# One bank for a head's output and its transpose, separate tiles for transposed parts, other queue orders and a two-byte selection

## The chip, the cores and the metric

The kernel is one program on one core of a Trainium2 chip. The core has TensorE (PE, with its weight loads PEld), VectorE (DVE), ScalarE (ACT), GpSimd (POOL) and SyncE (SP), which issues most DMAs; each takes its own instructions in order. The metric is the device time of one execution in microseconds.

## The reference, cut to what matters

```python
h = rms_norm(x, norm_mix)                       # x is 1024 x 1024, f32
r_q, r_k, r_v, r_g, d_q, d_c, d_pe, d_g, i_q, i_k, i_w = split(h @ w_in)
r_q, r_k = rotary(r_q), rotary(r_k)             # 8 heads of 64, theta 1e4
ret = head_group_norm(retention(r_q, r_k, r_v)) * silu(r_g)
c_kv = rms_norm(d_c, kv_norm)                   # latent of 128
k_pe, q_pe = rotary(d_pe), rotary(d_q[..., :16])
q_idx, k_idx = partial_rotary(i_q), partial_rotary(i_k)   # 8 heads of 32
# per block of 128 rows: indexer, selection, attention
rel = relu(einsum('bthd,bsd->bths', q_idx, k_idx) * 32 ** -0.5)
score = where(key chunk <= query chunk, einsum('bth,bths->bts', i_w * 8 ** -0.5, rel), -inf)
top_val, top_idx = top_k(score, 256)
prob = softmax of the logits on the 256 chosen keys (8 heads)
dsa = (prob @ c_kv chosen) @ w_uv * silu(d_g)
x = x + concat(ret, dsa) @ w_out
x = x + sigmoid(rms_norm(x, norm_ple) @ w_ple_gate) * (p @ w_ple_proj)
return rms_norm(x, norm_final)
```

## The kernel before

The 1024 rows are eight tiles of 128. Operands of the large products are split into a high part that ACT rounds and a low part that DVE or POOL subtracts, and three products are summed in PSUM. Instructions of an engine stand in an order that a scheduler has worked out ahead of the run; `mark(name, ins)` names an instruction and `behind(ins, name)` puts another one behind it.

First the projection for rotation and indexer runs (to 40 us of the span). From 40 to 97 us DVE and ACT make the rotation tables (`tables`, L350 to L359: a first table cosx, sinx and a second cosr, sinr, each with four DVE steps, the ACT Sin of L356, two more ACT steps and the DVE step of L359, then times `rstd_b` at L446). DVE rotates the indexer's operands (L426), splits them (L427 on ACT, L428), and SP writes the parts `ih`, `il` (L415, L419) and `xs` (L435, L436) to DRAM tensors `d_iq` and `d_ik`, and the rotated keys and attention queries to `d_qs` and `d_kp` (L440, L442). SP then loads `ks` (L459) and for each tile `qs` (L464, L465) from there. Meanwhile PE works on projection chunks (`n_chunk`, L502 to L504: chunk 2, 3, then 0, 1 and later 4, 5); ACT copies their bank out as `nst` (L506) and that frees the bank.

From 97 to 172 us PE forms the indexer's scores (L477), ACT the relu (L480) and DVE the weighted sum into `sc` (L482, L484), tiles 7, 6, 4, 2, 3, 5 in turn. From there to 375 us each row's threshold is searched: `Rows` holds tiles 2, 3 and 5 under the name a, which DVE counts (L657), and tiles 7, 6 and 4 under c, which ACT counts by the Sign of L673, a count for each tile in each of 16 rounds, twice (on a 16-bit key and, after `narrow`, on the next 16 bits `place`). `choose` (L707 to L722) then makes the additive mask `bias` from the threshold with five DVE passes over the scores of a tile: equal (L718), a running count (L719), the first few equals (L720), greater plus those (L721), and the scaling to 0 and -1e30 (L722). PE has chunks 4 and 5 and retention's transposes beside it.

Attention runs from 375 to 625 us. `prep_k` (L768 to L779) and `prep_v` make keys `kk` and values `vd` per head; L956 forms logits in the banks `lg`, L958 adds `bias` and takes the maximum, L961 and L962 (exp) follow, `key_chunks` transposes the weights on PE (L979), splits them into a tile `t2` of two halves (ACT L985 for the high, DVE L986 for the low), and `by_dim` multiplies them with the values into an `oo` bank (L1014, L1015), copies that bank with ACT to `os` (L1017), and transposes `os` back into the other `oo` bank (L1020), from which DVE sums (L1021). Two banks carry the name `oo`, taken in turn. The order places retention's units between the heads. From 625 us the gate's product follows, with x transposed to `xT` tiles of two halves (L1189, L1190).

Of the kernel before, what the change touches and what calls it, by code (L numbers as in the profile page):

```python
# [153 lines left out]
def _body(ctx, nc, tc, ap, dbg):  # L154
# [5 lines left out]
    marks = {}  # L160

    def behind(ins, mark):

        marks.setdefault(mark, []).append(ins)
# [184 lines left out]
    def tables(cos_t, sin_t):  # L349
        ang, kk = cos_t, sin_t  # L350
        first = V.tensor_scalar(kk, ang, 1.0 / (2.0 * math.pi), MAGIC, op0=OP.mult, op1=OP.add)
        V.tensor_scalar(kk, kk, -MAGIC, None, op0=OP.add)
        for c in CODY:
            V.scalar_tensor_tensor(ang, kk, -c, ang, op0=OP.mult, op1=OP.add)
        last = V.tensor_scalar(ang, ang, PI_LO, -PI_LO, op0=OP.min, op1=OP.max)
        sin = A.activation(sin_t, ang, AF.Sin)  # L356
        A.activation(cos_t, ang, AF.Sin, scale=0.5)
        A.activation(cos_t, cos_t, AF.Square)
        V.tensor_scalar(cos_t, cos_t, -2.0, 1.0, op0=OP.mult, op1=OP.add)  # L359
        return first, last, sin  # L360

    with tc.issue_after(squares.ins):
        angles(1, cosx)
        _, reduced, sine = tables(cosx, sinx)
        turn = angles(0, cosr)
# [23 lines left out]
    spread(rstd_b, rstd, "chunk 2 tile 0")  # L389
# [33 lines left out]
    for h in range(2):  # L423
        sl = slice(512 * h, 512 * h + 512)
        ma, mb = rotate(P1[h], cosx, sinx, h)
        turned = V.tensor_tensor(out=xo[:, :, sl], in0=two(ma), in1=two(mb), op=OP.add)  # L426
# [33 lines left out]
    for i in TI:  # L460
# [4 lines left out]
        Y.dma_start(f(qs)[64:96], d_iq[0, :, :, tsl])  # L465
# [19 lines left out]
        V.memset(sc[0:64, so + w - 64:so + w], -3.0e38)  # L485
# [5 lines left out]
    def n_chunk(c, func, place=nb):  # L491
        ws = [load_w(ap["w_n"][c, kg], 256) for kg in range(4)]
        for tg in range(2):
            for a in range(4):
# [11 lines left out]
                A.activation(st[:, a % 2], pb[:, a % 2], func, scale=rstd[:, j:j + 1])  # L506
# [70 lines left out]
    spread(cq, rkv)  # L577
# [58 lines left out]
    class Rows:  # L636
# [70 lines left out]
        def choose(self):  # L707
# [5 lines left out]
            V.tensor_scalar(need, self.count(sc, kf_, OP.is_gt), -1.0, 256.0, op0=OP.mult, op1=OP.add)  # L713
            for n, i in enumerate(self.tiles):
# [6 lines left out]
                V.scalar_tensor_tensor(eq, sc[:, KS[i]], kf_[:, n:n + 1], eq, op0=OP.is_gt, op1=OP.add)  # L721
                V.tensor_scalar(bias[:, SL[i]], eq, 1.0e30, -1.0e30, op0=OP.mult, op1=OP.add)  # L722
# [11 lines left out]

    onV, onA = Rows([2, 3, 5], "a", False).steps(), Rows([7, 6, 4], "c", True).steps()
# [233 lines left out]
    def key_chunks(pt, s0, last, split):  # L969
# [36 lines left out]
    def by_dim(i, h, pt, od):  # L1006
        ot = bank("oo")[:, :256]
# [160 lines left out]
    def tail_in(j):  # L1168
# [14 lines left out]
        for q in range(2):  # L1183
            pt = bank("tp")
            for k in range(4):
                T.transpose(pt[:, 128 * k:128 * k + 128], xt[:, 512 * q + 128 * k:512 * q + 128 * k + 128], ident)
            x2 = (dw_.tile([128, 2, 512], FR, name="xT", tag="t2") if q else
                  dq_.tile([128, 2, 512], FR, name="xT", tag="ql"))
            A.activation(x2[:, 0], pt, AF.Copy)  # L1189
            V.tensor_tensor(out=x2[:, 1], in0=pt, in1=f(x2)[:, 0], op=OP.subtract)  # L1190
# [69 lines left out]
```

## Time and profile before

| what | us |
|---|---|
| median of 3 runs | 807.86 |
| lowest and highest run | 806.78, 809.04 |
| profiled execution | 805.41 |
| span of its instructions | 803.6 |
| PE busy in it | 754.4 |
| DVE busy | 582.0 |
| ACT busy | 469.4 |

The profile shows one execution: the span counts from the first instruction to the last, and the execution's own time is 1.81 us more. Busy time of PE counts overlapping matmuls and is modelled at its ends, so a PE that is busy is not a PE at its peak. A timeline has one row for each run of alike instructions of an engine, with its start and length, and in brackets how long the engine stood idle ahead of it and what ended that. The list of waits sums such times by the pair of waiting and releasing line.

### The profile page before, as it was taken

What the parts mean: (1) busy time and instruction counts of PE and PEld (TensorE: products, weight loads), DVE (VectorE), ACT (ScalarE), POOL (GpSimd) and SP (SyncE); (2) the same over time, 40 slices, a digit from 0 to 9 for tenths busy, and PEclk for the clock granted to TensorE, in tenths of its full rate; (3) what the DMA queues carried; (4) which work ended last, traced back from release to release, by engine and by line L of the source; (5) the groups of instructions that cost most, each with busy time, mean ns of one, the idle gap of its engine ahead of it and who ended that gap; (6) DMA issues with size and microseconds to landing.
All of it is one profiled execution on the core that took longest, in us unless ns stands there. A gap on an engine that the chain in (4) does not pass through costs nothing.

```text
span 803.6 us, 12584 instructions
## 1 busy us (share of the span) xinstructions
PE 754.4 (94%) x4415; PEld 656.1 (82%) x4415; DVE 582.0 (72%) x1254; ACT 469.4 (58%) x1025; POOL 311.9 (39%) x237
## 2 busy tenths in 40 slices
PE   9999699989999999998999989799999899999995
PEld 6888599879888887997888879588788687888885
DVE  4968489999997999999879778755754633255344
ACT  6543466729997899963756656744754321333232
POOL 2918325455666434710046557630312230411000
PEclk9999899999999999999999999999999999999998
DMA  9414815323333224604525454654533662131201
GB/s 317 122 28 127 240 48 131 91 55 94 117 117 119 80 66 135 210 28 131 131 66 153 159 150 115 207 174 108 178 123 91 220 211 95 61 112 66 79 26 53
DMA packets 60831, 97.11 MB, mean 121 GB/s; under 512 B 5376, under 2 KB 32384, under 8 KB 60768
## 3 DMA queue, kind: packets, MB, share of 16 engines
q1 hardware_dynamic: 57152, 89.76, 36.5%
q10 hardware_dynamic: 3616, 6.55, 2.3%
q8 instruction: 35, 0.57, 0.3%
q14 instruction: 28, 0.23, 0.1%
HBM read 67.06 MB, written 29.23 MB: 120 GB/s over the span
## 4 chain that ended last, share of the span: by engine, by line
PE 53%; DVE 20%; issue 11%; DMA 7%; POOL 4%; ACT 3%; SPq 2%; POOLq 0%; ACTq 0%; DVEq 0%
PE lg L1165 6%; PE ra L1165 5%; PE big L326 3%; PE big L325 3%; PE big L324 3%; PE oo L1165 3%; DVE res L657 3%; PE nb L502 2%; PE nb L503 2%; PE nb L504 2%; DMA qk<-d_f 2%; PE ra L1122 2%; PE ra L1123 2%; PE ra L1124 2%; DVE sc L484 2%
## 5 line engine op out<-in xcount | busy, mean ns | idle before, releaser
L237 POOL TENSOR_TENSOR wlo<-wraw,whi 128x512 fp32r<-128x512 f32 (+1 forms) x58 | 88.8, 1547 | 66.2 <-ACT whi L236 66.2
L673 ACT ACTIVATE ajunk<-key,cthr 128x1024 bf16<-128x1024 int16 (+5 forms) x96 | 95.5, 994 | 14.8 <-DVE key L634 10.5
L502 PE MATMUL nb<-whi,xhi 128*128 128x256 f32 x256 | 74.8, 295 | 8.8 <-ACT nst L506 8.8
L657 DVE TENSOR_SCALAR_CACHE_REDUCE res<-key,athr 128x384 f32<-128x384 int16 (+5 forms) x96 | 75.5, 786 | 2.1
L503 PE MATMUL nb<-wlo,xhi 128*128 128x256 f32 x256 | 74.1, 291 | 0.7 <-POOL wlo L237 0.7
L504 PE MATMUL nb<-whi,xlo 128*128 128x256 f32 x256 | 73.5, 290 | 0.0
L335 POOL TENSOR_TENSOR rs_y<-rs_a,mhalf 128x1 f32<-128x1 f32 (+1 forms) x26 | 26.2, 1006 | 101.5 <-DVE rs_a L334 98.7
L962 ACT ACTIVATE lm<-lm,mxv 128x896 f32<-128x896 f32 (+3 forms) x64 | 49.5, 775 | 25.6 <-DVE mxv L961 25.4
L985 ACT ACTIVATE t<-tp 128x512 fp32r<-128x512 f32 (+1 forms) x72 | 39.3, 556 | 39.5 <-PE oo L1015 27.1
L502 PEld LDWEIGHTS nb<-whi,xhi 128*128 128x128 f32 x256 | 50.7, 199 | 10.8 <-ACT nst L506 9.7
L325 PE MATMUL big<-xlo,whi 128*128 128x512 f32 x144 | 56.1, 389 | 0.0
L324 PE MATMUL big<-xhi,whi 128*128 128x512 f32 x144 | 55.7, 389 | 0.0
L986 DVE TENSOR_TENSOR t<-tp,t 128x512 fp32r<-128x512 f32 (+1 forms) x72 | 45.6, 640 | 14.0 <-ACT t L985 13.6
L326 PE MATMUL big<-xhi,wlo 128*128 128x512 f32 x144 | 55.7, 390 | 0.0
L484 DVE SCALAR_TENSOR_TENSOR sc<-rel,wi,sc 128x1024 f32<-128x1024 f32 (+5 forms) x42 | 51.0, 1213 | 5.8 <-ACT rel L480 3.1
L958 DVE CUSTOM_DVE_ANT_0 lm<-lg,bias 128x512 f32<-128x512 f32 (+2 forms) x64 | 36.7, 587 | 23.5 <-PE tp L979 12.0
L503 PEld LDWEIGHTS nb<-wlo,xhi 128*128 128x128 f32 x256 | 50.8, 199 | 1.9 <-POOL wlo L237 1.3
L504 PEld LDWEIGHTS nb<-whi,xlo 128*128 128x128 f32 x256 | 50.4, 198 | 0.6
L979 PE MATMUL tp<-cst,lm 128*128 128x128 f32 x288 | 48.1, 277 | 0.6 <-DVE rs_a L334 0.3
L1014 PE MATMUL oo<-t,vd 128*128 128x256 f32 (+1 forms) x144 | 40.5, 293 | 7.7 <-ACT os L1017 6.2
L1219 DVE SCALAR_TENSOR_TENSOR sqx<-sqx,oo 128x512 f32<-128x512 f32 (+1 forms) x17 | 10.5, 653 | 49.6 <-PE oo L1165 35.0
L236 ACT ACTIVATE whi<-wraw 128x512 fp32r<-128x512 f32 (+1 forms) x58 | 34.9, 609 | 14.9 <-POOL cg L535 4.2
(492 smaller groups left out, 2423.5 us busy)
## 6 DMA issues: line engine op xcount, KB each, us to landing
wraw<-in_w_t SPq DMA_DIRECT2D x26, 256.0 KB, 2.7
wraw<-in_w_n SPq DMA_DIRECT2D x24, 256.0 KB, 2.6
d_f<-o SPq DMA_DIRECT2D x8, 512.0 KB, 3.9
qk<-d_f SPq DMA_DIRECT2D x8, 512.0 KB, 4.5
ql<-d_qs SPq DMA_DIRECT2D x16, 256.0 KB, 5.1
qh<-d_qs SPq DMA_DIRECT2D x32, 128.0 KB, 4.1
twr<-in_w_out SPq DMA_DIRECT2D x8, 512.0 KB, 5.4
xt<-in_x SPq DMA_DIRECT2D x8, 512.0 KB, 3.5
```

The lines of the kernel that those rows point to most:

```text
L237: G.tensor_tensor(out=lo, in0=raw, in1=f(hi), op=OP.subtract)
L324: T.matmul(outs[h], wh, xhi[k][:, sl], start=k == 0, stop=False)
L325: T.matmul(outs[h], wh, xlo[k][:, sl], start=False, stop=False)
L326: last = T.matmul(outs[h], wl, xhi[k][:, sl], start=False, stop=k == 7)
L484: V.scalar_tensor_tensor(dst, rel[:, :w], wi[:, i, h:h + 1], dst, op0=OP.mult, op1=OP.add)
L502: T.matmul(pb[:, a % 2], xhi[k][:, tsl], wh, start=k == 0, stop=False)
L503: T.matmul(pb[:, a % 2], xhi[k][:, tsl], wl, start=False, stop=False)
L504: last = T.matmul(pb[:, a % 2], xlo[k][:, tsl], wh, start=False, stop=k == 7)
L657: V.tensor_scalar(junk, src[:, KS[i]], thr[:, n:n + 1], 0.0, op0=op, op1=OP.add, accum_out=cnt[:, n:n + 1])
L673: A.activation(junk[:, :128 * (i + 1)], src[:, KS[i]], AF.Sign, bias=self.thr[:, n:n + 1], accum_out=cnt[:, n:n + 1])
L962: A.activation(lm[:, :w], lm[:, :w], AF.Exp, bias=mx, scale=0.125, accum_out=den[:, a, h:h + 1])
L1165: T.matmul(po[c.start // 512][:, c.start % 512:c.start % 512 + c.stop - c.start], a, b[:, c], start=k == 0 and m == 0, stop=k == n - 1 and ...
```

## The change

- The stores of `xs` to `d_qs` and `d_kp` and part of the DRAM work stand behind the load of the first tile's queries on SP ("first queries").
- The second table's first DVE step stands behind the last `xs` subtract; its Sin stands behind the last copy of chunk 3 ("chunk 3 copied 7"); its last three DVE steps stand behind the scoring of tile 4 ("scored 4").
- `spread` of rstd stands behind tile 1 of chunk 2 (it was tile 0), and that of the kv norm behind "block 10".
- One Sign of the first round (tile 6) stands behind a copy of chunk 1.
- In `choose` the count of the greater ones writes its 0 or 1 as bf16 into the memory of `key`; L721, which compared f32 scores again, becomes an add of two bf16 tiles (L730 in the new file), and L722 leaves DVE for an ACT Identity (new L731) with `out_of`, a column of -1e30 that one POOL memset fills.
- `by_dim` takes one bank for a head: the output in columns 0 to 255, the transpose in 256 to 511; `os` is 256 wide. `t2` becomes three tiles `th` and two tiles `tl`; three of the `xT` pairs in the tail use them.

DVE has six scaled compares fewer and six adds more, and six scalings fewer; ACT has six more; PE and SP have as many instructions as before.

```diff
     def behind(ins, mark):
-        marks.setdefault(mark, []).append(ins)
+        if mark in marked:
+            queue(ins, marked[mark])
+        else:
+            marks.setdefault(mark, []).append(ins)
...
-    spread(rstd_b, rstd, "chunk 2 tile 0")
+    spread(rstd_b, rstd, "chunk 2 tile 1")
...
-        (V if h else G).tensor_tensor(out=xs[1][:, :, sl], in0=xo[:, :, sl], in1=f(xs[0])[:, :, sl], op=OP.subtract)
+        parts = (V if h else G).tensor_tensor(out=xs[1][:, :, sl], in0=xo[:, :, sl], in1=f(xs[0])[:, :, sl], op=OP.subtract)
...
-            Y.dma_start(d_qs[n, :, 8 * x:8 * x + 8].rearrange("b j h t -> (j h) b t"),
-                        f(xs[n])[0:64, x].rearrange("p (b t) -> p b t", t=256))
-        Y.dma_start(d_kp[n].rearrange("(x j) t -> j x t", x=2), f(xs[n])[104:112])
-    first, *_ = tables(cosr, sinr)
-    queue(first, turned)
+            behind(Y.dma_start(d_qs[n, :, 8 * x:8 * x + 8].rearrange("b j h t -> (j h) b t"),
+                               f(xs[n])[0:64, x].rearrange("p (b t) -> p b t", t=256)), "first queries")
+        behind(Y.dma_start(d_kp[n].rearrange("(x j) t -> j x t", x=2), f(xs[n])[104:112]), "first queries")
+    first, _, sine, cosine = tables(cosr, sinr)
+    queue(first, parts)
+    behind(sine, "chunk 3 copied 7")
+    behind(cosine, "scored 4")
     for t in (cosr, sinr):
-        V.tensor_tensor(out=t, in0=t, in1=rstd_b, op=OP.mult)
+        behind(V.tensor_tensor(out=t, in0=t, in1=rstd_b, op=OP.mult), "scored 4")
...
-    spread(cq, rkv)
+    spread(cq, rkv, "block 10")
...
+                    if bit == 15 and n == 1 and src is key:
+                        behind(ins, "chunk 1 copied 3")
...
+            above = key.bitcast(BF)
-            V.tensor_scalar(need, self.count(sc, kf_, OP.is_gt), -1.0, 256.0, op0=OP.mult, op1=OP.add)
+            V.tensor_scalar(need, self.count(sc, kf_, OP.is_gt, above), -1.0, 256.0, op0=OP.mult, op1=OP.add)
...
-                V.scalar_tensor_tensor(eq, sc[:, KS[i]], kf_[:, n:n + 1], eq, op0=OP.is_gt, op1=OP.add)
-                V.tensor_scalar(bias[:, SL[i]], eq, 1.0e30, -1.0e30, op0=OP.mult, op1=OP.add)
+                V.tensor_tensor(out=above[:, KS[i]], in0=above[:, KS[i]], in1=eq, op=OP.add)
+                A.activation(bias[:, SL[i]], above[:, KS[i]], AF.Identity, scale=1.0e30, bias=out_of)
...
-        t2 = dw_.tile([128, 2, 512], FR, name="t2")
-        th, tl_ = t2[:, 0], t2[:, 1]
+        th = tl_ = dw_.tile([128, 512], FR, name="th", bufs=3)
         if split:
+            tl_ = dw_.tile([128, 512], FR, name="tl")
...
-        ot = bank("oo")[:, :256]
+        both = bank("oo")
+        ot = both[:, :256]
...
-        os_ = dw_.tile([128, 512], F32, name="os")[:, :256]
+        os_ = dw_.tile([128, 256], F32, name="os")
         A.activation(os_, ot, AF.Copy)
-        tbp = bank("oo").rearrange("p (j d) -> p j d", d=128)
+        tbp = both[:, 256:].rearrange("p (j d) -> p j d", d=128)
```

The first place is SP's queue between the last `d_iq` store of the low parts and the first queries `qs`. Before:

```order
26 L415 DMA d_iq<-il 64x1024
27 L419 DMA d_ik<-il 24x1024
28 L440 DMA d_qs<-xs_520 64x4x256 x2
29 L442 DMA d_kp<-xs_520 8x2x1024
30 L459 DMA ks<-d_ik 32x1024 x3
31 L521 DMA d_g_88<-nst 128x2x128
32 L521 DMA d_g_89<-nst 128x2x128
33 L415 DMA d_iq<-ih 128x1024
34 L521 DMA d_g_88<-nst 128x2x128
35 L521 DMA d_g_89<-nst 128x2x128
36 L233 DMA wraw<-in_w_n 128x512
37 L464 DMA qs<-d_iq 64x8x128
```

Now, where L418, L422, L464, L469, L470 and L443 are the old L415, L419, L459, L464, L465 and L440:

```order
26 L418 DMA d_iq<-il 64x1024
27 L422 DMA d_ik<-il 24x1024
28 L464 DMA ks<-d_ik 32x1024 x2
29 L469 DMA qs<-d_iq 64x8x128
30 L464 DMA ks<-d_ik 32x1024
31 L470 DMA qs<-d_iq 32x8x128
32 L443 DMA d_qs<-xs_519 64x4x256 x2
33 L445 DMA d_kp<-xs_519 8x2x1024
34 L443 DMA d_qs<-xs_520 64x4x256 x2
35 L445 DMA d_kp<-xs_520 8x2x1024
```

Nine DMAs and the three `ks` loads stood between the low parts' stores and the first queries' load; now only the `ks` loads do, one of them between its two halves. The six stores to `d_qs` and `d_kp`, which all stood ahead of the queries, now come behind them, and the `ih` store of row 33 stands ahead of the piece shown.

The second place is ACT's queue in the last three rounds of the second search (`ajunk` is the Sign's output, `cthr` and `csg` its small steps). Before, from the 896 wide Sign of the third round from the end:

```order
440 L673 ACTIVATE ajunk,ccnt<-key,cthr 128x896
441 L676 ACTIVATE csg<-ccnt,coff 128x1
442 L836 ACTIVATE kk_4552<-qk 128x512
443 L841 ACTIVATE qz_4555<-qk 64x4x128 x2
444 L506 ACTIVATE nst<-lg,rstd 128x256
445 L524 DMA d_dg<-nst 128x2x256
446 L673 ACTIVATE ajunk,ccnt<-key,cthr 128x640
447 L676 ACTIVATE csg<-ccnt,coff 128x1
448 L678 ACTIVATE cthr<-csg,cthr 128x1
```

Now, with L679 the Sign and L731 the new Identity:

```order
429 L731 ACTIVATE bias<-key,out_of 128x384
430 L684 ACTIVATE csg<-ccnt,coff 128x1
431 L679 ACTIVATE ajunk,ccnt<-key,cthr 128x896
432 L530 DMA d_dg<-nst 128x2x256
433 L512 ACTIVATE nst<-ra,rstd 128x256
434 L731 ACTIVATE bias<-key,out_of 128x512
435 L686 ACTIVATE cthr<-csg,cthr 128x1
436 L679 ACTIVATE ajunk,ccnt<-key,cthr 128x640
437 L684 ACTIVATE csg<-ccnt,coff 128x1 x2
438 L679 ACTIVATE ajunk,ccnt<-key,cthr 128x1024
439 L686 ACTIVATE cthr<-csg,cthr 128x1
440 L731 ACTIVATE bias<-key,out_of 128x768
```

The masks of tiles 2, 3 and 5 (384, 512 and 768 wide) now stand between the Signs of c, the last of them with two Signs of its round and the whole last round behind it.

The third place is DVE's queue at the end of the selection of tile 4 (640 wide), where the first key products `kk` are subtracted. Before:

```order
377 L718 TENSOR_SCALAR junk<-sc,ckfin 128x640
378 L719 SCALAR_TENSOR_TENSOR res<-junk 128x640
379 L720 SCALAR_TENSOR_TENSOR junk<-res,cneed,junk 128x640
380 L721 SCALAR_TENSOR_TENSOR junk<-sc,ckfin,junk 128x640
381 L722 TENSOR_SCALAR bias<-junk 128x640
382 L779 TENSOR_TENSOR kk_4365<-oo,kk_4365 64x512
383 L779 TENSOR_TENSOR kk_4365<-tp,kk_4365 64x512
```

Now, where L727 to L730 are the old L718 to L721 and L790 the old L779:

```order
379 L727 TENSOR_SCALAR junk<-sc,ckfin 128x640
380 L728 SCALAR_TENSOR_TENSOR res<-junk 128x640
381 L790 TENSOR_TENSOR kk_4361<-oo,kk_4361 64x512
382 L790 TENSOR_TENSOR kk_4361<-tp,kk_4361 64x512
383 L729 SCALAR_TENSOR_TENSOR junk<-res,cneed,junk 128x640
384 L790 TENSOR_TENSOR kk_4362<-oo,kk_4362 64x512
385 L790 TENSOR_TENSOR kk_4362<-tp,kk_4362 64x512
386 L730 TENSOR_TENSOR key<-key,junk 128x640
```

The subtracts of the first two heads' keys move ahead of the last one or two steps of the selection.

## Rows read from the trace of the kernel before

**Rows 1.** The page's head and its totals: busy time, share of the span and instructions.

```profile
span 803.6 us, 12584 instructions
PE 754.4 (94%) x4415; PEld 656.1 (82%) x4415; DVE 582.0 (72%) x1254; ACT 469.4 (58%) x1025; POOL 311.9 (39%) x237
```

**Rows 2.** Stretches of the span: length, then busy time and instructions of PE, PEld, DVE, ACT and POOL, granted clock of TensorE, DMA share, GB/s.

```profile
40.00:97.00 57.00, 46.90 (x331) 43.88 (x330) 38.48 (x35) 23.84 (x35) 28.71 (x20) 0.97 0.46 123
...
375.00:530.00 155.00, 140.85 (x953) 125.16 (x953) 125.89 (x315) 99.84 (x186) 76.21 (x69) 0.96 0.51 150
```

**Rows 3.** What PE waited for over the whole span: line and releaser, us in total, times, longest.

```profile
PE nb L502 <- ACT nst L506: 8.8, 3, 5.1
PE oo L1014 <- ACT os L1017: 6.2, 4, 3.2
...
PE oo L760 <- DVE kk L779: 2.3, 1, 2.3
...
PE ib L371 <- issue: 1.6, 1, 1.6
```

**Rows 4.** Timelines of PE and ACT between 78 and 98 us: start, length, engine and line.

```profile
84.78 0.58 PE L502 MATMUL nb<-whi,xhi 128*128 128x256 f32 x1 [5.08 <-ACT nst L506]
96.71 1.17 PE L477 MATMUL big<-ks,qs 96*128 96x512 f32 x4 [3.20 <-DMA qs<-d_iq]
```

```profile
83.31 1.06 ACT L356 ACTIVATE sinr<-cosr 128x1024 f32<-128x1024 f32 x1 [5.36 <-DVE cosr L355]
```

**Rows 5.** Timeline of DVE between 69 and 98 us.

```profile
69.99 2.89 DVE L351 TENSOR_SCALAR sinr<-cosr 128x1024 f32<-128x1024 f32 x1
...
72.92 1.67 DVE L352 TENSOR_SCALAR sinr<-sinr 128x1024 f32<-128x1024 f32 x1
74.51 3.42 DVE L428 TENSOR_TENSOR xs<-xo,xs 128x1024 fp32r<-128x1024 f32 x1
...
84.39 1.23 DVE L446 TENSOR_TENSOR sinr<-sinr,rstd_b 128x1024 f32<-128x1024 f32 x1 [1.12 <-ACT sinr L356]
88.07 0.94 DVE L359 TENSOR_SCALAR cosr<-cosr 128x1024 f32<-128x1024 f32 x1 [2.45 <-ACT cosr L358]
89.05 2.20 DVE L446 TENSOR_TENSOR cosr<-cosr,rstd_b 128x1024 f32<-128x1024 f32 x1
```

**Rows 6.** SP's queue of DMAs between 80 and 93 us, and POOL's `il`, which its first row stores.

```profile
80.53 0.92 SPq L415 DMA_DIRECT2D d_iq<-il  x1
...
87.95 0.49 SPq L415 DMA_DIRECT2D d_iq<-ih  x1
...
91.24 0.56 SPq L464 DMA_DIRECT2D qs<-d_iq  x1
91.84 1.13 SPq L465 DMA_DIRECT2D qs<-d_iq  x1
```

```profile
74.00 2.85 POOL L252 TENSOR_TENSOR il<-it,ih 128x1024 fp32r<-128x1024 f32 x1
```

**Rows 7.** The end of the scoring: length, DVE's busy time and instructions, granted clock, DMA share, GB/s.

```profile
150.00:172.00 22.00, 21.81 (x23) 1.00 0.33 91
```

**Rows 8.** Timeline of DVE in the selection: tiles 2, 3 and 5 of a, then 7, 6 and 4 of c, and the first key subtract.

```profile
339.93 1.57 DVE L721 SCALAR_TENSOR_TENSOR junk<-sc,akfin,junk 128x384 bf16<-128x384 f32 x1
...
345.59 0.75 DVE L721 SCALAR_TENSOR_TENSOR junk<-sc,akfin,junk 128x512 bf16<-128x512 f32 x1
...
352.24 1.94 DVE L721 SCALAR_TENSOR_TENSOR junk<-sc,akfin,junk 128x768 bf16<-128x768 f32 x1
...
354.49 0.16 DVE L683 TENSOR_SCALAR cv<-cthr 128x3 int32<-128x3 f32 x1
...
362.57 1.28 DVE L721 SCALAR_TENSOR_TENSOR junk<-sc,ckfin,junk 128x1024 bf16<-128x1024 f32 x1
363.89 0.43 DVE L722 TENSOR_SCALAR bias<-junk 128x1024 bf16<-128x1024 bf16 x1
...
372.05 0.89 DVE L720 SCALAR_TENSOR_TENSOR junk<-res,cneed,junk 128x640 bf16<-128x640 f32 x1
372.97 0.89 DVE L721 SCALAR_TENSOR_TENSOR junk<-sc,ckfin,junk 128x640 bf16<-128x640 f32 x1
373.89 0.33 DVE L722 TENSOR_SCALAR bias<-junk 128x640 bf16<-128x640 bf16 x1
374.25 0.69 DVE L779 TENSOR_TENSOR kk<-oo,kk 64x512 fp32r<-64x512 f32 x1
```

**Rows 9.** Timeline of ACT in the last three rounds of c: the Signs by width and the last small step.

```profile
337.88 1.03 ACT L673 ACTIVATE ajunk<-key,cthr 128x896 bf16<-128x896 uint16 x1
...
341.28 0.82 ACT L673 ACTIVATE ajunk<-key,cthr 128x640 bf16<-128x640 uint16 x1
...
344.51 1.03 ACT L673 ACTIVATE ajunk<-key,cthr 128x896 bf16<-128x896 uint16 x1
...
352.93 0.48 ACT L678 ACTIVATE cthr<-csg,cthr 128x1 f32<-128x1 f32 x2
```

**Rows 10.** Attention: PE's timeline at two heads' starts, and from ACT's list of waits between 375 and 640 us the weight split of L1064 (line and releaser, us in total, times, longest).

```profile
411.74 0.39 PE L1014 MATMUL oo<-t,vd 128*128 128x256 f32 x1 [1.51 <-ACT os L1017]
...
473.99 0.39 PE L1014 MATMUL oo<-t,vd 128*128 128x256 f32 x1 [0.90 <-ACT os L1017]
```

```profile
ACT wo3h L1064 <- DMA twr<-in_w_out: 2.9, 1, 2.9
```

More of the change, by code (lines that the diff above doesn't have):

```diff
@@ L172, in mark @@
     def mark(name, ins):
+        marked[name] = ins
         for x in marks.pop(name, []):
@@ L358, in tables @@
         A.activation(cos_t, cos_t, AF.Square)
-        V.tensor_scalar(cos_t, cos_t, -2.0, 1.0, op0=OP.mult, op1=OP.add)
-        return first, last, sin
+        return first, last, sin, V.tensor_scalar(cos_t, cos_t, -2.0, 1.0, op0=OP.mult, op1=OP.add)
     with tc.issue_after(squares.ins):
         angles(1, cosx)
-        _, reduced, sine = tables(cosx, sinx)
+        _, reduced, sine, _ = tables(cosx, sinx)
         turn = angles(0, cosr)
@@ L425, in _body @@
         ma, mb = rotate(P1[h], cosx, sinx, h)
-        turned = V.tensor_tensor(out=xo[:, :, sl], in0=two(ma), in1=two(mb), op=OP.add)
+        V.tensor_tensor(out=xo[:, :, sl], in0=two(ma), in1=two(mb), op=OP.add)
         A.activation(xs[0][:, :, sl], xo[:, :, sl], AF.Copy)
-        (V if h else G).tensor_tensor(out=xs[1][:, :, sl], in0=xo[:, :, sl], in1=f(xs[0])[:, :, sl], op=OP.subtract)
+        parts = (V if h else G).tensor_tensor(out=xs[1][:, :, sl], in0=xo[:, :, sl], in1=f(xs[0])[:, :, sl], op=OP.subtract)
         pw = big()
@@ L464, in _body @@
         Y.dma_start(f(qs)[0:64], d_iq[:, :, :, tsl].rearrange("n r h t -> (n r) h t"))
-        Y.dma_start(f(qs)[64:96], d_iq[0, :, :, tsl])
+        mark("queries" if i != TI[0] else "first queries", Y.dma_start(f(qs)[64:96], d_iq[0, :, :, tsl]))
         so = OFF[i] - OFF[2]
@@ L484, in _body @@
                 V.scalar_tensor_tensor(dst, rel[:, :w], wi[:, i, h:h + 1], dst, op0=OP.mult, op1=OP.add)
-        V.memset(sc[0:64, so + w - 64:so + w], -3.0e38)
+        mark(f"scored {i}", V.memset(sc[0:64, so + w - 64:so + w], -3.0e38))
     ix.close()
@@ L505, in n_chunk @@
                 mark(f"chunk {c} tile {j}", last)
-                A.activation(st[:, a % 2], pb[:, a % 2], func, scale=rstd[:, j:j + 1])
+                mark(f"chunk {c} copied {j}",
+                     A.activation(st[:, a % 2], pb[:, a % 2], func, scale=rstd[:, j:j + 1]))
                 if a % 2 == 0:
@@ L651, in start, with count @@
             G.memset(self.thr, -at if self.scalar else at)
-        def count(self, src, thr, op):
+        def count(self, src, thr, op, out=None):
             cnt = self.small("cnt")
             for n, i in enumerate(self.tiles):
-                junk = tkp.tile([128, S], F32, name="res")[:, :128 * (i + 1)]
+                junk = tkp.tile([128, S], F32, name="res")[:, :128 * (i + 1)] if out is None else out[:, KS[i]]
                 V.tensor_scalar(junk, src[:, KS[i]], thr[:, n:n + 1], 0.0, op0=op, op1=OP.add,
@@ L672, in bit @@
                     junk = tkp.tile([128, S], BF, name="ajunk", bufs=1)
-                    A.activation(junk[:, :128 * (i + 1)], src[:, KS[i]], AF.Sign, bias=self.thr[:, n:n + 1],
-                                 accum_out=cnt[:, n:n + 1])
+                    ins = A.activation(junk[:, :128 * (i + 1)], src[:, KS[i]], AF.Sign, bias=self.thr[:, n:n + 1],
+                                       accum_out=cnt[:, n:n + 1])
+                    if bit == 15 and n == 1 and src is key:
+                        behind(ins, "chunk 1 copied 3")
                 for n in range(self.n):
@@ L733, in steps @@
                 yield
+    out_of = tkp.tile([128, 1], F32, name="out_of", bufs=1)
+    G.memset(out_of, -1.0e30)
     onV, onA = Rows([2, 3, 5], "a", False).steps(), Rows([7, 6, 4], "c", True).steps()
@@ L987, in key_chunks @@
         else:
-            th = f(t2)[:, s0 // 2 % 2]
+            th = f(th)
             A.activation(th[:, :o], tp[:, :o], AF.Copy)
@@ L1186, in tail_in @@
                 T.transpose(pt[:, 128 * k:128 * k + 128], xt[:, 512 * q + 128 * k:512 * q + 128 * k + 128], ident)
[L1187 to L1190, printed above, removed]
+            if q:
+                xh, xl = (dw_.tile([128, 512], FR, name="xT" + tag, tag=tag, bufs=n) for tag, n in (("th", 3), ("tl", 2)))
+            else:
+                x2 = dq_.tile([128, 2, 512], FR, name="xT", tag="ql")
+                xh, xl = x2[:, 0], x2[:, 1]
+            A.activation(xh, pt, AF.Copy)
+            V.tensor_tensor(out=xl, in0=pt, in1=f(xh), op=OP.subtract)
             for k in range(4):
-                hi.append(x2[:, 0, 128 * k:128 * k + 128])
-                lo.append(x2[:, 1, 128 * k:128 * k + 128])
+                hi.append(xh[:, 128 * k:128 * k + 128])
+                lo.append(xl[:, 128 * k:128 * k + 128])
         return xt, sq, r1, p2, hi, lo
```

2 lines of the change are left out of this document (1 added, 1 removed).

## The prediction

> **What bounds the kernel now.** I read the totals first: PE is busy for 754.4 of 803.6 us [rows 1], so a change that only spares DVE or ACT work pays where PE, or what PE comes to wait for, is held by it. [...] The third is the list of what PE waits for: 8.8 us for ACT's copy of a chunk bank, 6.2 us for `os`, 2.3 us for the first key subtract, 1.6 us for the issue of the spread of rstd [rows 3]. The timelines tell what those waits hang on, and here the reader should look at who stood in front of the releaser. ACT's Sin was idle 5.36 us for DVE's last table step and began at 83.31; the copy that PE needed stood behind it, so PE stood 5.08 us until 84.78. Then PE came to the first score and stood 3.20 us more for the queries, until 96.71 [rows 4]. At the end of the scoring DVE is busy 21.81 of 22.00 us, so DVE sets that end [rows 7]. In the selection of c DVE works without a hole from 354.49, just behind ACT's last small step at 352.93 [rows 9], to the key subtract at 374.25 [rows 8] that ends PE's wait.
>
> **Up to the first score.** Two DVE steps of the second table, 2.89 and 1.67 us, ran ahead of the `xs` subtract [rows 5]; they now follow it. With the four stores of the second halves gone from the front of SP's queue, the last part the queries need is `il`. It ended at 76.85 (74.00 plus 2.85), but its store was issued only at 80.53 [rows 6]. The spread of rstd now follows one more tile of chunk 2; it waited 1.6 us anyway, and I let `il` come 1 us later, at 77.9. Its two stores are then issued to about 79.4, the second from 78.8. From issue of a store to the load that waits for it took 3.3 us (87.95 to 91.24), and from the second queries' load to the first score 4.87 us (91.84 to 96.71) [rows 4, 6]. So 78.8 + 3.3 + 0.7 for the `ks` load in between + 4.9 gives 87.7. PE itself, free of the 5.08, 3.20 and 1.6 us, would be there at 86.8, so nothing earlier is to be had but by the clock. The first score moves by 9.0 us; from one more landing (6) to the earlier PE with its clock held (11).
>
> **What that costs later.** DVE's last three table steps leave a stretch where it was idle for a stretch where it is the bound: 0.94, 1.23 and, for the second product, 1.23 to 2.20 us [rows 5], 3.4 to 4.4 in all; I take 4. The Sin and its two followers fall into ACT time that has holes in the scoring. So the scoring ends, and both searches begin, 9 - 4 = 5 us earlier. A wait for a copy behind a Sign (in the other 3.7 of the 8.8 us in rows 3) may go as well, but what ends the selection is not PE, so I count it at nothing. The other spread ("block 10") has about as many transposes in front of it as before: nothing.
>
> **The selection.** Two things run against each other. First, ACT. The three masks of a now stand between the Signs of c. In the old times ACT comes to the first at 337.9 (the 896 Sign) and must wait until DVE's step at 339.93 is done, say 340.5; the mask itself costs about 0.6 us, between nothing and the 0.82 of the 640 wide Sign [rows 8, 9]. That is 3.2 us. The second waits for a step that began at 345.59, now about 1.7 us sooner, where ACT is at 344.5: 0.9 us more. The third stands ahead of the 896 Sign that began at 344.51 and is at its place at about 348.5, and waits for the step that began at 352.24, sooner by the savings on the first two tiles (1.3 + 0.3 + 0.4 + 0.3), so near 350.6; with its own 0.9 us that Sign begins at 351.5, 7.0 us late. Behind it are the rest of that round and one whole round, 344.51 to 353.4: ACT ends near 360.4 and DVE's `cv` begins 6.0 us late, at 360.5. Second, DVE's own chain from `cv` to the key subtract, 19.76 us, loses the three scalings (0.43 + about 0.4 + 0.33), saves on three adds, and has the last L720 (0.89) and the last add behind the subtract [rows 8]. No row shows an add of two bf16 tiles: it lies between a scaling (0.43 at 1024 wide) and the compare that it replaces (1.28). I take half the compare, since it has two tensor inputs as that has and two bytes as the scaling has: 3.3 us becomes 1.7. So 19.76 - 1.1 - 1.6 - 1.3 = 15.8, and the subtract begins at 376.3 on the old clock, 2.0 us later than before. If ACT never waited it would be 4.0 us earlier; at the old prices of the compares and with every step of a as slow as before, 6.8 later (`cv` near 364.3 and 16.8 of chain). [...]
>
> **Attention and tail.** Of the 6.2 us that PE waited for `os`, two waits (1.51, 0.90) are a head whose first product needs the bank that the head before still holds [rows 3, 10]. With a bank of its own for every head in turn this is gone, since the transpose no longer takes the second bank. The longest, 3.2 us, is not of this kind alone: ACT stood 2.9 us for a DMA of `wo3` [rows 10], ahead of its copy; the next head no longer needs that copy, but transposes of the old head do, so I count it only in the bound. That makes 3.0 us. The clock's 0.96 over 155 us [rows 2] is some 6 us; which of its falls follow these waits the rows don't tell, and I give a third, 2 us. So 5 us, from nothing (the next wait, the maximum of the logits, stands right behind) to 9. Three `th` tiles against two pairs spare ACT waits, not PE's. The `xT` tiles in the tail: nothing, as PE has work there and waits for other lines.
>
> **The sum.** The profiled execution took 805.41 us; 805.4 - 9 + 4 + 2 - 5 = 797.4. The median of the runs is 2.45 us above that execution, so 799.9 by it.
>
> **Rivals.** *The gain comes whole.* ACT's masks don't hold the Signs, because DVE's a steps come sooner than I make them or ACT had slack, and all `os` waits go with their clock falls: 805.4 - 11 + 3.4 - 4 - 9 = 784.8, median 787.3. For it: two of the three compares of a, 1.57 and 1.94 us, stand far above what their width asks [rows 8], and adds may not; against it: the order in which ACT's rows stand. *The banks change nothing.* In attention each wait for `os` is followed by a wait for the next logits, and the time goes there: 802.4, median 804.9, which a measurement can hardly tell from no change. *Slower: the masks hold ACT's queue.* One mechanism, at 338 to 351 us: ACT takes its instructions in order, and a mask that waits for DVE stops the Signs, whose end DVE then waits for. At the upper price the key subtract comes 6.8 us late; it decides as soon as the first score's lead, less the tables, is under that: with 6 - 4.4 = 1.6 of lead and an attention that gains nothing, 805.4 - 1.6 + 6.8 = 810.6, median 813.1. The compare of 384 wide that took 1.57 us against 0.75 for 512 wide [rows 8] shows that a DVE step there can cost twice its price, which feeds this case. [...]
>
> **How the numbers follow.** Forecast 0.50, whole gain 0.22, no gain from the banks 0.16, slower 0.12. About 0.3% (2.4 us) is what a measurement of this kernel can tell from no change, so faster means below 805.4. Faster: nearly all of the first two and half of the third, 0.79; same: the rest of the third and the edge of the others, 0.10; slower 0.11. The range runs from 786, which cuts off the better half of the whole gain (some 0.10), to 808, which cuts off most of the slower case (0.10).
>
> **What would show it.** The first score near 88 us in place of 96.71, with no ACT Sin ahead of it; the three DVE table steps after tile 4's scoring; an end of the scoring 5 us earlier. In the selection three holes in ACT of some 2.6, 0.3 and 2 us ahead of the masks, and a hole on DVE ahead of `cv`; adds of 1024 wide between 0.43 and 1.28 us. In attention the pair of L1014 and `os` gone from PE's list of waits, and the clock above 0.96. I am wrong if the queries land no earlier, if ACT shows no hole there, or if the attention's stretch is as long as before.

## The result and the profile after

| what | before | after |
|---|---|---|
| median of 4 runs, us | 807.32 | 797.37 |
| lowest and highest | 804.48, 809.04 | 794.67, 799.03 |
| span of the profiled execution | 803.6 | 797.2 |

The ratio is 0.987, with a 95% interval from 0.982 to 0.992: about 10 us faster, clear of noise, and 2.5 us from the 799.9 that was forecast. The two profiled executions, 805.41 and 799.03 us, lie 6.4 us apart, so the stages below account for that much. But the stages did not share the time out as forecast. Three points of the two traces show it: PE's first key product, the last logits, and the end. One execution of experiment 1, the profiled one, ran at a granted clock of 0.65 and took 1038.33 us; it is left out of the times below.

Timeline of PE before, the first key product and the last logits (its wait is in [rows 3]):

```profile
375.00 0.79 PE L760 MATMUL oo<-uvh,ckh 128*128 128x512 f32 x1 [2.26 <-DVE kk L779]
...
620.87 0.28 PE L957 MATMUL lg<-kk,ql 128*128 128x256 f32 x1
```

The same two after the change:

```profile
381.90 0.50 PE L771 MATMUL oo<-uvh,ckh 128*128 128x512 f32 x1 [2.26 <-DVE kk L790]
...
614.75 0.29 PE L968 MATMUL lg<-kk,ql 128*128 128x256 f32 x1
```

Up to the key product the changed kernel loses 6.9 us. From there to the last logits it takes 232.85 us (614.75 less 381.90) instead of 245.87, so it wins 13.0. From there to the end it takes 182.5 us instead of 182.7. The sum is the 6.4 us between the spans.

**The start.** Timeline of PE after the change, in the stretch that ends with the first score:

```profile
50.93 0.58 PE L507 MATMUL nb<-whi,xhi 128*128 128x256 f32 x1 [3.46 <-ACT nst L512]
...
56.21 1.56 PE L374 MATMUL ib<-cst,rstd 128*128 128x128 f32 x11
...
92.84 1.16 PE L482 MATMUL big<-ks,qs 96*128 96x512 f32 x4 [1.14 <-DMA qs<-d_iq]
```

The old waits of 5.08 and 3.20 us [rows 4] are gone or down to 1.14, yet the first score is only 3.9 us earlier. The first row is new: the chunk matmuls that now stand ahead of the spread (the second row) need a bank that ACT copies out with rstd as its scale. PE waits 3.46 us for that copy, and then runs them at a granted clock of 0.50, from 52 to 56 us. The stretches (columns as in [rows 2]) show it and, at the end of the scoring, DVE still the bound:

```profile
40.00:97.00 57.00, 51.64 (x356) 48.39 (x356) 34.82 (x32) 22.43 (x32) 30.26 (x21) 0.94 0.38 105
...
52.00:56.00 4.00, 4.00 (x21) 4.00 (x20) 0.00 (x0) 0.00 (x0) 0.00 (x0) 0.50 0.00 0
...
150.00:172.00 22.00, 21.52 (x166) 20.62 (x165) 21.72 (x24) 8.81 (x18) 17.26 (x9) 1.00 0.27 90
375.00:530.00 155.00, 144.01 (x1020) 130.12 (x1019) 134.05 (x336) 109.85 (x205) 78.93 (x70) 0.99 0.54 160
```

The three table steps in the scoring (timeline of DVE after) cost 0.62 + 2.06 + 1.21, that is 3.9 us:

```profile
135.12 0.62 DVE L363 TENSOR_SCALAR cosr<-cosr 128x1024 f32<-128x1024 f32 x1
135.67 2.06 DVE L451 TENSOR_TENSOR sinr<-sinr,rstd_b 128x1024 f32<-128x1024 f32 x1
137.98 1.21 DVE L451 TENSOR_TENSOR cosr<-cosr,rstd_b 128x1024 f32<-128x1024 f32 x1
...
168.37 0.11 DVE L490 MEMSET sc<- 64x64 f32 x1
```

The last row ends the scoring. Before it was

```profile
169.12 0.11 DVE L485 MEMSET sc<- 64x64 f32 x1
```

so 0.75 us are left of the lead.

**The selection.** Timeline of ACT after: a Sign of the third round from the end, and the masks of tiles 2, 3 and 5 (compare [rows 9]):

```profile
339.30 1.13 ACT L679 ACTIVATE ajunk<-key,cthr 128x1024 bf16<-128x1024 uint16 x1
...
345.73 0.62 ACT L731 ACTIVATE bias<-key,out_of 128x384 bf16<-128x384 bf16 x1 [2.28 <-DVE key L730]
...
349.95 0.72 ACT L731 ACTIVATE bias<-key,out_of 128x512 bf16<-128x512 bf16 x1 [2.03 <-DVE key L730]
...
354.76 0.93 ACT L731 ACTIVATE bias<-key,out_of 128x768 bf16<-128x768 bf16 x1 [1.40 <-DVE key L730]
```

Each mask stopped ACT for DVE, 5.7 us in all. Timeline of DVE after (compare [rows 8]):

```profile
345.35 0.34 DVE L730 TENSOR_TENSOR key<-key,junk 128x384 bf16<-128x384 bf16 x1
...
365.78 0.17 DVE L691 TENSOR_SCALAR cv<-cthr 128x3 int32<-128x3 f32 x1 [11.06 <-ACT cthr L686]
...
373.68 0.69 DVE L730 TENSOR_TENSOR key<-key,junk 128x1024 bf16<-128x1024 bf16 x1
...
381.15 0.69 DVE L790 TENSOR_TENSOR kk<-oo,kk 64x512 fp32r<-64x512 f32 x1
```

DVE, which had no hole here before, stands 11.06 us for ACT's last small step. Its own chain is short: 15.4 us from `cv` to the key subtract, where it was 19.76, and an add 1024 wide takes 0.69 us.

**Attention.** PE's list of waits between 375 and 530 us (columns as in [rows 3]), the wait for the maximum `mxv` before:

```profile
PE lg L956 <- DVE mxv L958: 3.7, 4, 1.7
```

and the list after:

```profile
PE oo L1026 <- ACT th L996: 2.9, 2, 1.5
PE oo L771 <- DVE kk L790: 2.8, 2, 2.3
PE ra L888 <- DVE x L867: 1.8, 3, 0.9
...
PE lg L967 <- DVE mxv L969: 0.8, 2, 0.4
```

The pair with `os`, 6.2 us of [rows 3], is gone, the clock is 0.99 in place of 0.96 (last stretch above), and there is a second change: the wait of the logits for `mxv` is 0.8 us in place of 3.7. The stretches from key product to last logits, before and after (columns as in [rows 2]):

```profile
375.00:620.87 245.87, 230.61 (x1503) 203.43 (x1504) 175.42 (x476) 146.91 (x307) 92.46 (x80) 0.97 0.47 141
```

```profile
381.90:614.75 232.85, 224.12 (x1506) 200.25 (x1507) 173.06 (x482) 149.04 (x311) 92.78 (x80) 0.99 0.49 148
```

PE's idle time falls from 15.3 to 8.7 us and the busy time of as many matmuls from 230.6 to 224.1, at a granted clock of 0.99 in place of 0.97: half of the 13.0 us is less waiting, half is shorter busy time.

### The profile page after: what moved, and what is told of

It is laid out like the page before. It is cut to its first block, busy times and chain, and to the rows that moved or that the text cites. A ratio compares the mean times of both kernels' runs of the same rounds, so it can differ in the third digit from the quotient of the medians.

```text
span 797.2 us, 12581 instructions
## 1 busy us (share of the span) xinstructions
PE 752.3 (94%) x4415; PEld 656.7 (82%) x4415; DVE 576.9 (72%) x1248; ACT 474.1 (59%) x1031; POOL 314.0 (39%) x238
## 4 chain that ended last, share of the span: by engine, by line
PE 39%; DVE 7%; DMA 5%; ACT 2%; issue 1%; POOL 0%; SPq 0%; POOLq 0%; DVEq 0%
PE lg L1177 6%; PE ra L1177 5%; PE ra L1136 3%; PE ra L1134 3%; PE ra L1135 3%; PE oo L1177 3%; PE tp L990 3%; PE lg L967 2%; PE lg L968 1%; PE oo L1027 1%; PE oo L1026 1%; DMA twr<-in_w_gate 1%; PE ra L904 1%; DVE qz L853 1%; DMA d_mix<-og 1%
## 5 line engine op out<-in xcount | busy, mean ns | idle before, releaser
L679 ACT ACTIVATE ajunk<-key,cthr 128x1024 bf16<-128x1024 int16 (+5 forms) x96 | 95.4, 993 | 16.0 <-DVE key L640 9.5
L996 ACT ACTIVATE th<-tp 128x512 fp32r<-128x512 f32 (+1 forms) x72 | 40.0, 558 | 38.5 <-PE tp L990 37.3
L973 ACT ACTIVATE lm<-lm,mxv 128x896 f32<-128x896 f32 (+3 forms) x64 | 49.5, 774 | 22.4 <-DVE mxv L972 20.1
L997 DVE TENSOR_TENSOR tl<-tp,th 128x512 fp32r<-128x512 f32 (+1 forms) x72 | 45.8, 639 | 7.4 <-ACT th L996 5.0
L1026 PE MATMUL oo<-th,vd 128*128 128x256 f32 (+1 forms) x144 | 40.5, 289 | 2.9 <-ACT th L996 2.9
L1027 PE MATMUL oo<-tl,vd 128*128 128x256 f32 (+1 forms) x144 | 40.2, 312 | 0.0
```

Source lines behind the costliest of these rows:

```text
L679: ins = A.activation(junk[:, :128 * (i + 1)], src[:, KS[i]], AF.Sign, bias=self.thr[:, n:n + 1], accum_out=cnt[:, n:n + 1])
```

## The experiments

Times are medians; the kernel before ran beside each group (806.4, 807.8 and 806.9 us). Line numbers are those of each kernel.

**1. The spread.** In the changed kernel, one word:

```diff
-    spread(rstd_b, rstd, "chunk 2 tile 1")
+    spread(rstd_b, rstd, "chunk 2 tile 0")
```

> The changed kernel with one edit taken back: the spread of rstd stands behind tile 0 of chunk 2 again. Theory: tile 1 first needs a bank that ACT copies out only when rstd is known, so the spread (56.21 us in the changed kernel, 49.39 before) came 6.8 us late and pushed all vector work of this stage; with tile 0 the spread is near 49.4, the first score 5 to 7 us earlier than 92.84, the scoring ends near 162, and the time falls by 4 to 7 us below the changed kernel's 797.4, to 790.5 to 793.5. Rival: SP's stores and loads set the first score, not the vector work; then it stays within 1.5 us of 92.84 and the time within 2 us of 797.4.

Measured: 794.0 us, ratio to before 0.984 (0.982 to 0.986). That is 3.4 us under the changed kernel: the theory's direction, less than its 4 to 7. The stages are read in another kernel with the same edit:

**2. The early part alone**, with the spread behind tile 0; the choice and the attention are those of before. SP's order, the Sign behind chunk 1 and the spread of the kv norm behind "block 10" are in it too; none of them was tried by itself.

> The changed kernel with the choice and the attention of before, and the spread of rstd behind tile 0: the early part alone, without its worst step. Theory: the first score comes 5 to 8 us before 96.7, the scoring ends 2 to 5 us earlier (the table steps on DVE take 3.4 to 4.4 back), and the time is 802 to 804.5. Rival: what is won up to the scoring is lost in the two searches, whose ACT order changes with it; then within 2.4 us of 806.4.

Measured: 802.93 us, ratio 0.995 (0.992 to 0.998). Timelines of PE and of DVE in it:

```profile
49.39 0.79 PE L374 MATMUL ib<-cst,rstd 128*128 128x128 f32 x5 [1.66 <-issue]
...
88.10 1.17 PE L482 MATMUL big<-ks,qs 96*128 96x512 f32 x4 [1.01 <-DMA qs<-d_iq]
```

```profile
163.92 0.11 DVE L490 MEMSET sc<- 64x64 f32 x1
...
372.39 0.69 DVE L787 TENSOR_TENSOR kk<-oo,kk 64x512 fp32r<-64x512 f32 x1
```

The spread is 6.8 us earlier than in the changed kernel (49.39 against 56.21), the first score 4.7 (88.10 against 92.84) and the scoring ends 5.2 before that of the kernel before. At the first key subtract 1.9 us are left of it (372.39 against 374.25 in [rows 8]). So the spread set the first score, as the theory had it (8.6 us before that of the kernel before, a little over its 8), and the time is the theory's; but most of the lead is lost in the searches, as the rival had it, though not by ACT's order.

The trace shows where. `cv` follows DVE's search of a without a hole, as before (353.91 against 354.49), so DVE sets it; ACT's search is done 1.8 us earlier. From the end of the scoring to the end of that search (the second `av`, 335.25 against 334.55) DVE takes 171.3 us where it took 165.4. The search has one small step `ad` in each of its 32 rounds. DVE's list of lines (count, us in total, mean ns, idle) before and in this run:

```profile
L666 DVE TENSOR_SCALAR ad<-acnt 128x3 bf16<-128x3 f32 x32 | 14.0, 438 | 0.7
```

```profile
L672 DVE TENSOR_SCALAR ad<-acnt 128x3 bf16<-128x3 f32 x32 | 19.8, 620 | 0.8
```

The median of these steps is 0.17 us in both. The 11 of this run that took more than 0.4 us all stood beside a POOL instruction and ended within 0.04 us of the end of one, such as this pair of timelines:

```profile
206.23 1.85 DVE L672 TENSOR_SCALAR ad<-acnt 128x3 bf16<-128x3 f32 x1
```

```profile
205.64 2.41 POOL L541 TENSOR_TENSOR cg<-cosr,gam 128x1024 f32<-128x1024 f32 x1
```

The new order puts more of them there: the 32 steps take 19.4 to 20.1 us in all seven kernels that have the early part (the changed one, experiments 2, 3 and 8 to 11) and 14.0 to 15.8 in the five without it. That POOL's work holds these steps is read from the rows; no run moved that work away.

**3. The masks.** In the changed kernel the three masks are put behind c's search:

```diff
-                    A.activation(new[:, n:n + 1], sg[:, n:n + 1], AF.Identity, scale=-half, bias=self.thr[:, n:n + 1])
+                    ins = A.activation(new[:, n:n + 1], sg[:, n:n + 1], AF.Identity, scale=-half, bias=self.thr[:, n:n + 1])
+                if bit == 0 and src is place:
+                    mark("searched", ins)
...
-                A.activation(bias[:, SL[i]], above[:, KS[i]], AF.Identity, scale=1.0e30, bias=out_of)
+                ins = A.activation(bias[:, SL[i]], above[:, KS[i]], AF.Identity, scale=1.0e30, bias=out_of)
+                if not self.scalar:
+                    behind(ins, "searched")
```

> The changed kernel with the three ACT masks of tiles 2, 3 and 5 put behind the last small step of c's search; the work is the same, only ACT's order differs. Theory: the masks held the Signs; without them ACT has no wait for a key of L730 before 358 us, DVE's cv comes 6 to 8 us sooner than 365.78, the key subtract near 374, and the time falls by 4 to 7 us, to 790.5 to 793.5. Rival: PE's own work (it waited only 2.3 us for that subtract) is the bound there, and the time falls by at most 2.5 us.

Measured: 790.63 us, ratio 0.981 (0.978 to 0.983), 6.7 us under the changed kernel, as the theory had it. Timeline of DVE in it:

```profile
354.67 0.17 DVE L693 TENSOR_SCALAR cv<-cthr 128x3 int32<-128x3 f32 x1
...
371.48 0.69 DVE L794 TENSOR_TENSOR kk<-oo,kk 64x512 fp32r<-64x512 f32 x1
```

No hole is left ahead of `cv`, which comes 11.1 us earlier with the same work on every engine. Of that, 2.1 us are there already at the 1024 Sign of the third round from the end (337.25 against 339.30), ahead of the first mask; from that Sign to `cv` it is 17.4 us in place of 26.5, so the masks' place costs 9.1.

**4. The changed choice alone**, on the kernel before (bf16 add, ACT masks in the scheduler's order).

> The kernel before with the changed choice alone (two-byte add on DVE, masks by ACT in the order the scheduler gives). Theory: the masks hold ACT's Signs, DVE stands 5 to 11 us ahead of cv, the key subtract is 2 to 7 us later than 373.9 and the time 808 to 813. Rival: the DVE work that is spared pays, the subtract comes earlier and the time is 801 to 804.

Measured: 806.78 us, ratio 1.000 (0.998 to 1.002). The expected hole is there, on DVE:

```profile
361.92 0.17 DVE L683 TENSOR_SCALAR cv<-cthr 128x3 int32<-128x3 f32 x1 [9.97 <-ACT cthr L678]
...
380.80 0.69 DVE L782 TENSOR_TENSOR kk<-oo,kk 64x512 fp32r<-64x512 f32 x1 [2.10 <-ACT kk L780]
```

and the key subtract stands at 380.80, 6.6 us late, but the medians show neither the loss of the theory nor the gain of the rival. In the profiled executions 4.2 us of the loss are left at the end (spans of 807.8 and 803.6), since the part behind the last logits is 2.5 us shorter; this execution lies 2.9 us over its median, that of before 1.9 under its own, which is as far as executions of one kernel differ. More is not settled.

**5. The bank alone**, on the kernel before:

```diff
-        ot = bank("oo")[:, :256]
+        both = bank("oo")
+        ot = both[:, :256]
...
-        os_ = dw_.tile([128, 512], F32, name="os")[:, :256]
+        os_ = dw_.tile([128, 256], F32, name="os")
...
-        tbp = bank("oo").rearrange("p (j d) -> p j d", d=128)
+        tbp = both[:, 256:].rearrange("p (j d) -> p j d", d=128)
```

> The kernel before with one part of the change alone: a head's output and its transpose in one bank, os 256 wide. Theory: the waits for os go (6.2 us in the list of waits become under 1), with some of the clock, and PE's waits from 400 to 525 us fall by 5 to 9 us; time 798 to 803 against 807.3. Rival: the separate tiles are what pays in attention, or the next wait takes the place; then this kernel is within 2.4 us of 807.3.

Measured: 789.14 us, ratio 0.978 (0.976 to 0.980). This one edit is 8 us better than the whole change. Its timeline of PE, and its list of waits between 375 and 530 us:

```profile
377.39 0.50 PE L760 MATMUL oo<-uvh,ckh 128*128 128x512 f32 x1 [2.14 <-DVE kk L779]
...
611.17 0.28 PE L957 MATMUL lg<-kk,ql 128*128 128x256 f32 x1
```

```profile
PE oo L1015 <- ACT t L985: 3.7, 2, 2.8
...
PE lg L956 <- DVE mxv L958: 0.5, 2, 0.3
```

From key product to last logits it takes 233.8 us, 12.1 less than before, and from there to its end (span 788.9) 177.7, 5.0 less. No row has `os`, and the wait for `mxv` fell to 0.5 us, although nothing of `mxv` was edited. Both rivals fall. In the traces of all kernels attention takes 231.9 to 235.3 us in the eight with one bank per head and 242.6 to 246.1 in the four with two.

**6. The separate tiles alone**, on the kernel before, with `os` 256 wide to make room (in the tail eight of the sixteen `xT` pairs become such tiles, not three):

```diff
-        t2 = dw_.tile([128, 2, 512], FR, name="t2")
-        th, tl_ = t2[:, 0], t2[:, 1]
+        th = tl_ = dw_.tile([128, 512], FR, name="th", bufs=3)
         if split:
+            tl_ = dw_.tile([128, 512], FR, name="tl")
```

> The kernel before with the other part of the attention alone: three tiles th and two tiles tl in place of the pairs t2 (and the xT pairs in the tail), os 256 wide to make room, two banks per head as before. Theory: it spares waits of ACT, not of PE; the os waits stay near 6 us, and the time is within 2.4 us of 807.3. Rival: most of the 12 us that the changed kernel gained in attention comes from here; then 797 to 803.

Measured: 800.01 us, ratio 0.991 (0.988 to 0.993). Neither: it gained 6.4 us, but not where the rival said. Its key product starts at 378.25 and its last logits at 620.80, so attention gains 3.3 us, and the last part (to its span of 797.9) 5.6. The waits for `os` did not stay near 6 us: between 375 and 530 us they add up to 2.4, those for `mxv` to 2.5. But they are not gone, though `os` is 256 wide here too, so that width alone is not what the bank's edit won.

**7. Both together**, on the kernel before:

> The kernel before with both attention parts: one bank per head and the separate tiles th and tl (and the xT pairs). Theory: the bank carries the gain and the tiles add nothing to it; time within 2.5 us of the 789.1 of the bank alone. Rival: the tiles' 6.4 us adds up; then near 783.

Measured: 793.77 us, ratio 0.984 (0.981 to 0.988): 4.6 us slower than the bank alone (the kernel before was 1.4 us slower beside this group), outside what theory and rival gave. The traces show the same: attention is alike (234.2 and 233.8 us), the part behind the last logits takes 182.2 us in place of 177.7. With the bank there, the tiles cost.

**8. Both repairs in the changed kernel:** the edits of 1 and 3.

> The changed kernel with both repairs: the spread behind tile 0 and the three masks behind c's search. Theory: the two waits lie one behind the other, so the gains add: 797.4 - 3 - 6, that is 787 to 789.5. Rival: PE's own work between 170 and 375 us is the bound once one of them is gone; then 790 to 791.5, as the masks alone gave.

Measured: 788.61 us, ratio 0.977 (0.973 to 0.980): the repairs nearly add (3.4 and 6.7 became 8.8).

**9. The same with the pairs `t2` of before** (the edit of 6 and that of the `xT` pairs taken back).

> Both repairs (the spread behind tile 0, the three masks behind c's search), the bank per head, the changed choice, but the pairs t2 of before in place of the tiles th and tl. Theory: the tiles add nothing to the banks (793.8 with them and 789.1 without, on the kernel before), so this is as fast as the 788.6 with tiles or up to 4 us faster: 784.5 to 789. Rival: with three high tiles ACT runs further ahead and the repaired kernel needs that; then 791 to 795.

Measured: 782.12 us, ratio 0.969 (0.966 to 0.972). It is faster than the theory's best, 15 us under the changed kernel and the fastest of all. The difference to 8 lies in the last part. PE from 600 to 640 us in experiment 8, and its wait there:

```profile
600.00:640.00 40.00, 35.99 (x184) 29.45 (x183) 23.25 (x44) 14.00 (x25) 12.92 (x6) 0.96 0.64 208
```

```profile
619.83 0.50 PE L1138 MATMUL ra<-wo0h,mTh 128*128 128x512 f32 x1 [3.28 <-DVE mTl L1129]
```

and in experiment 9:

```profile
600.00:640.00 40.00, 38.70 (x206) 32.46 (x205) 20.68 (x39) 13.88 (x25) 12.48 (x6) 1.00 0.62 227
```

```profile
617.30 0.50 PE L1138 MATMUL ra<-wo0h,mTh 128*128 128x512 f32 x1 [1.29 <-DVE mTl L1129]
```

With the tiles PE waits 2.0 us longer for DVE's `mTl`, and the granted clock is 0.96 in place of 1.00; the changed kernel has the same wait, 3.32 us at 632.24. Ahead of `mTl` in DVE's queue stands a pair of products, in experiment 8 beside a subtract of POOL, in experiment 9 not:

```profile
615.74 3.43 DVE L1048 TENSOR_TENSOR od<-od,gd 128x512 f32<-128x512 f32 x2
```

```profile
615.80 2.82 POOL L1081 TENSOR_TENSOR wg0l<-twr,wg0h 128x1024 fp32r<-128x1024 f32 x1 [8.24 <-ACT wg0h L1080]
```

```profile
613.60 1.29 DVE L1048 TENSOR_TENSOR od<-od,gd 128x512 f32<-128x512 f32 x2
```

The pair takes 3.43 or 3.44 us in all five kernels that have both the tiles and the bank, and 1.28 or 1.29 in the seven others: the 2.1 us are as long as PE's extra wait. So part of the tiles' cost is that the order that comes with them puts these products beside POOL; this is read from the rows, and the rest of the 4.5 us by which the last part differs is open.

**10. The early part with the spread behind tile 0, and the bank**, with the choice of before and the pairs.

> The early part with the spread behind tile 0, and the bank per head; the choice and the pairs t2 are those of before. Theory: the two gains lie in different stretches and add: 789.1 - 4 = 785, so 783 to 787. Rival: the early gain is lost again before attention, as the key subtract of the early part alone came only 2.4 us earlier; then 787 to 790.

Measured: 788.54 us, ratio 0.977 (0.974 to 0.979): the rival. The early lead adds next to nothing to the bank as long as the old choice follows it: of the 4.6 us by which the scoring ends before that of the kernel before, 1.2 are left at the key product (373.80 against 375.00). Against experiment 9, which differs by the changed choice with late masks, that choice is worth 6.4 us.

**11. The masks scaled on DVE** from the two-byte sum, with the spread behind tile 0:

```diff
-                A.activation(bias[:, SL[i]], above[:, KS[i]], AF.Identity, scale=1.0e30, bias=out_of)
+                V.tensor_scalar(bias[:, SL[i]], above[:, KS[i]], 1.0e30, -1.0e30, op0=OP.mult, op1=OP.add)
```

> The changed kernel with the spread behind tile 0, and the masks scaled on DVE as before (from the two-byte sum) in place of ACT's Identity. Theory: it is the place of the masks in ACT's queue that costs, not who does them; DVE's chain has 1.1 us more than with late masks, so the time is 788 to 791 against 788.6. Rival: DVE, the bound of the selection, pays for all six scalings; then 792 or more.

Measured: 789.22 us, ratio 0.978 (0.975 to 0.980), 0.6 us from late masks on ACT. The theory holds: what the masks cost was their place in ACT's queue, not their work. Nor does the relief of DVE show by itself, since 0.6 us is within the noise.

## Why the prediction came out, step by step

- **The first score: wrong by the spread.** The step "I let `il` come 1 us later" was mis-sized. The spread came 6.8 us later and POOL's `il` ended at 82.55 (79.17 and 3.38 of length) in place of 77.9. What I left out is that the matmuls put ahead of the spread need a bank whose copy waits for the same rstd. The rest of that sum came out: with the spread back behind tile 0 (experiment 2) `il` ended at 77.4 and the first score came at 88.1, where 77.9 and 87.7 were worked out.
- **The table steps: right.** 3.9 us measured, 4 taken; in experiment 2, with the spread repaired, the scoring ended 5.2 us earlier, against 5.
- **The masks in ACT's queue: right in mechanism and near in size.** Holes of 2.28, 2.03 and 1.40 us were measured for 2.6, 0.3 and 2. From the 1024 Sign of the third round from the end to `cv` the changed kernel takes 26.5 us (339.30 to 365.78), where before it took 20.1 (the same Sign stood at 334.37 and `cv` at 354.49): 6.4 us for a forecast of 6.0. Experiment 3 shows the mechanism; there the same stretch is 9.1 us shorter, in part because in the new order some of ACT's other copies already stand ahead of that Sign.
- **DVE's chain: right.** 15.4 us for 15.8, adds of c 1.8 us (0.69 + 0.62 + 0.49) for 1.7. An f32 product of 1024 took 1.21 us (the table steps above), the two-byte add 0.69. Beside these adds POOL ran nothing (in the changed kernel, between 342.97 and 358.04 and between 360.55 and 390 us); other DVE steps did take longer beside POOL (1.85 us for a median of 0.17, 3.43 for 1.29, in experiments 2 and 9).
- **The lead up to there: wrong.** The step "So the scoring ends, and both searches begin, 9 - 4 = 5 us earlier" was carried to the key subtract as if nothing but the masks could change the searches' length. In experiment 2 5.2 us became 1.9 without any mask in ACT's queue, since DVE's search of a took 5.9 us longer and its steps from there to the subtract 2.6 less. In the changed kernel it took 6.0 longer (its second `av` at 339.82 against 334.55, though the scoring had ended 0.75 early), and the 1024 Sign on ACT was 4.9 us late before the first mask stood in front of it. From ACT's first Sign of the second search to this one it was 74.2 us in place of 70.3; 1.9 of the 3.9 us are copies (`kk`, `qz`) that before stood behind it. So the subtract came 4.9 + 6.4 - 4.4 (DVE's shorter chain) = 6.9 us late. The slower rival had named 6.8, but that it is so near is luck: its mechanism took place, and it had not named the 4.9.
- **Attention: right in mechanism, mis-sized.** 13.0 us against 5, and over the upper bound of 9. Both terms were too small: 3.0 us of waits against 6.5 less idle time of PE, 2 us of clock against 6.5 less busy time. I counted the `os` waits themselves, and took the maximum of the logits as the next wait, right behind. With the bank alone the wait for `mxv` between 375 and 530 us went from 3.7 us in the kernel before to 0.5. The sum that reads the transposed head stands in DVE's queue, as the maximum does; that the one held the other is an argument from the rows, not an experiment.
- **The tail: no change, as forecast** (0.2 us), but by luck: the bank alone won 5.0 us there, and the tiles beside it lost 4.5 (experiments 5 and 7). The step "The `xT` tiles in the tail: nothing" was wrong.

So the total was met by luck, because two misses offset each other: some 10 us too much hoped for up to attention, 8 too little in it.

## What to carry to other kernels

An instruction moved behind a mark takes on every wait of what then stands ahead of it: look for one that needs the moved instruction's own source, as the copy that needed rstd (the spread came 6.8 us late). Work handed to an engine with spare time stops that engine's queue if it waits for the engine that it relieves (the masks: 5.7 us of holes on ACT, 9.1 us on the way to `cv`); put it behind the chain that others wait for. When a double use of two banks makes them one, count the waits of the next engines in the same queues too (that for `mxv` went from 3.7 to 0.5 us), and try each part of a bundle by itself, since here one of its parts alone was faster than the whole (789.14 against 797.37 us). When a new order loses what it won, compare the length of the same instructions in both traces, and look for what another engine ran beside the longer ones (POOL beside an `ad` of 1.85 us, where the median is 0.17).

## What was not expected

The tiles `th` and `tl` gain 6.4 us on the kernel before and cost 4.6 and 6.5 us where each head has its own bank (experiments 5 to 9). The wait of 3.3 us of PE in the last part is in all five kernels that have both the tiles and the bank, and in no other (0.4 to 1.3 us). The early part, which ends the scoring 5.2 us sooner, gives most of it back on DVE, in small steps that stand beside POOL (19.8 us in all in place of 14.0, experiment 2).
